# All matrix products of a three-layer network as whole float32 matmuls, with weights packed tile by tile

## The chip, the cores and the metric

The kernel runs on one core of a Trainium2 chip. The metric is the device time of one execution in microseconds (us). Before the change it is 1247.71 us, the median of 3 runs (1245.24 to 1251.49).

## The reference, cut to what matters

All data is float32: 256 tokens of width 1024, batch 1. There are seven sublayers; numbered by `s` in the kernel they are 0 to 6:

```
s=0 mixer_ab:  proj = h @ w_in_ab  (1024 x 2072); sparse + window attention, sink attention; y = o @ w_out
s=1, 3 ffn:    y = (silu(h @ w_gate) * (h @ w_up)) @ w_down          (1024 x 2816 twice, 2816 x 1024)
s=2 mixer_cd:  proj = h @ w_in_cd  (1024 x 2304); block attention, stick-breaking attention; y = o @ w_out
s=4, 6 ffn:    the same with other weights, residual factor 0.5
s=5 mixer_s5:  proj = h @ w_in_2   (1024 x 2048); gated convolution and a state space with a gate; y = o @ w_out_2
around each:   h = rms_norm(x) * (1 + scale) + shift;   x = x + gate * (norm of) y
               scale, shift, gate = c @ mod_w + mod_b    (21 vectors of 1024, each from a 1024 x 1024 matrix)
```

The products accumulate over a depth of 1024 (8 tiles of 128), in the last product of a feed-forward part over 2816 (22 tiles).

## The kernel before, in words

The activations `h` stay in SBUF, feature-major: 8 tiles of 128 features by 256 tokens. All weights are streamed once from HBM. SyncE issues nearly all loads on one queue, in order; a load waits there until its buffer is free. TensorE's instructions stand in the program's written order. The other engines' order is found by the framework's planner.

**Three passes.** Most products are made from parts. `split` (L170) takes a raw weight tile of 128x1024 and makes a high part `whi` on ScalarE (L184, type fp32r) and the rest, `wlo`, on VectorE (L185). `evac` (L110) does the same with the activations, as `hhi` and `hlo`. Then `mm3` (L100 to L108) adds three matmuls of fp32r operands: high by high, high by low, low by high. One call of `mm3` with low parts is thus three matmul instructions, of 128 stationary columns and 256 moving ones in the projections (`proj_a`, L225). `out_step` (L439) does the same with 512 moving columns in the feed-forward parts' last product (L449 to L451), and `tok_half` (L470) with token-major products (L480, L483).

**Whole products already there.** Where there are no low parts the operands are plain float32 and one matmul call is made: the attention mixers' output projections (L447, operands `raw` and `o`: 2 mixers x 8 depth tiles x 2 halves of the rows x 2 halves of the columns = 64 calls of 512 columns), the convolution's 12 column tiles in `mixer_s5` (L104, `h` and `raw`: 12 x 8 = 96 calls of 256 columns), the gate of the state space (L1529: 16 calls of 256 columns), its first inputs (L1360: 64 calls of 128 columns).

**Calls in three passes.** With 256 columns: the feed-forward parts' projections, 4 parts x 20 column tiles x 2 matrices x 8 = 1280, the projections of `mixer_ab` and `mixer_cd`, 13 column tiles x 8 = 104 each, together 1488; and the token-major first columns of the feed-forward parts, 4 x 2 halves x 2 matrices x 8 = 128. With 512 columns: 4 parts x 22 x 2 x 2 = 352 in the last products, 16 in `mixer_cd`, 16 in `mixer_s5`.

**Modulations.** `mod` (L285) accumulates `c @ mod_w` on VectorE, row tile by row tile (L252, tile `macc`), as background work that `plan` and `pay` (L138 to L152) spread over the feed-forward parts. `mod_part` (L261) splits the sum, and `mod_end` (L270) sums it over partitions with two matmuls of 512 columns (L276, L277); 19 vectors in two halves make 38.

**Buffers.** 4 raw weight buffers of 8 KB a partition, 4 of 4 KB for the modulations (`mraw`), 4 each of 4 KB for `whi` and `wlo`. Weights are loaded by columns, in runs of 512 to 2048 bytes, or by rows, in runs of 2048 or 4096. `chain` (L214) prepares one item (load and split) ahead of the item that runs.

**Boundaries.** At the end of a feed-forward part (`out_halves`, L516) the last four depth tiles run for the first half of the tokens, then for the second; under the second, the first half's norm is made and transposed (L365). `split_ahead` (L499) splits the next part's first weights.

Of the kernel before, what the change touches and what calls it, by code (L numbers as in the profile page):

```python
# [61 lines left out]

class Net:
    def __init__(self, ctx, tc, I, out, dbg=None):
        self.ctx, self.tc, self.nc, self.I, self.out, self.dbg = ctx, tc, tc.nc, I, out, dbg or {}
        self.bgq, self.late, self.wait = [], [], 0
        self.anchor = None
        self.nacc = 0
        self.nextra = 0
# [30 lines left out]
    def mm3(self, out, lh, ll, rh, rl, first, last):  # L100
        """float32 product: in three passes over parts, or, without low parts, as it is"""
        mm = self.nc.tensor.matmul
        if ll is None:
            mm(out, lh, rh, start=first, stop=last)  # L104
            return
        mm(out, lh, rh, start=first, stop=False)  # L106
        mm(out, lh, rl, start=False, stop=False)  # L107
        mm(out, ll, rh, start=False, stop=last)  # L108

    def evac(self, hi, lo, ps, scale=None):  # L110
        nc = self.nc
        if lo is None:
            nc.scalar.activation(hi, ps, AF.Copy, scale=1.0 if scale is None else scale)  # L113
        else:
# [23 lines left out]
    def plan(self, slots):  # L138
        """the waiting work, by its time, over steps of the given slack"""
# [26 lines left out]
    # ---------------------------------------------------------------- weights  # L166
    def raw(self):
        return self.wp.tile([128, 2048], F32, tag="raw", name="raw", bufs=4)

    def split(self, src, shape, pool=None):  # L170
        n = 1
        for s in shape:
            n *= s
        p, bufs = (self.wp, 4) if pool is None else (pool, self.nextra)
        hi = p.tile([128, 1024], F32R, tag="whi", name="whi", bufs=bufs)
        lo = p.tile([128, 1024], F32R, tag="wlo", name="wlo", bufs=bufs)

        def view(t):
            v = t[:, :n]
            if len(shape) == 2:  # L180
                return v.rearrange("p (a b) -> p a b", a=shape[0])
            return v.rearrange("p (a b c) -> p a b c", a=shape[0], b=shape[1])
        hv, lv = view(hi), view(lo)
        self.nc.scalar.activation(hv, src, AF.Copy)  # L184
        self.nc.vector.tensor_tensor(lv, src, hv.bitcast(F32), ALU.subtract)  # L185
        if len(shape) == 3:
            hv = hi[:, :n].rearrange("p (a b) -> p a b", a=shape[0])
            lv = lo[:, :n].rearrange("p (a b) -> p a b", a=shape[0])
        return hv, lv

    def load_cols(self, w, cols):
        """[1024, n] columns (a list of (start, stop)) -> raw [128, 8, total]"""
        tot = sum(b - a for a, b in cols)
        r = self.raw()
        v = r[:, :8 * tot].rearrange("p (k n) -> p k n", k=8)
        o = 0
        for a, b in cols:
            self.nc.sync.dma_start(out=v[:, :, o:o + b - a],
                                   in_=w[:, a:b].rearrange("(k p) n -> p k n", p=128))
            o += b - a  # L200
        return v

    def load_rows(self, w, r0, c0, c1):
        """rows r0 .. r0 + 511 of some columns -> raw [128, 4, n]"""
        r = self.raw()[:, :4 * (c1 - c0)].rearrange("p (k n) -> p k n", k=4)
        self.nc.sync.dma_start(out=r, in_=w[r0:r0 + 512, c0:c1].rearrange("(k p) n -> p k n", p=128))
        return r

    def weights(self, src, shape, xl, pool=None):
        """the weights as a product with x takes them: in parts if x is in parts"""  # L210
        return (src, None) if xl is None else self.split(src, shape, pool)
# [22 lines left out]
    def mod_start(self, w, b, c, grain):  # L234
        """b + c @ w, as partial sums over 128 partitions"""
# [7 lines left out]
        nc.sync.dma_start(out=acc[0:1, :], in_=b)  # L243
        wv = w.rearrange("(p k) n -> p k n", p=128)

        def piece(i):
            def run():
                for kk in range(grain * i, grain * i + grain):
                    r = self.wp.tile([128, D], F32, tag="mraw", name="mraw", bufs=4)
                    nc.sync.dma_start(out=r, in_=wv[:, kk, :])  # L250
                    with self.behind(kk == 0):
                        nc.vector.scalar_tensor_tensor(acc, r, c[:, kk:kk + 1], acc, ALU.mult, ALU.add)  # L252
            return run
        return acc, [piece(i) for i in range(8 // grain)]

    def behind(self, on):
        """behind the last part's norm on the vector engine"""
# [3 lines left out]
    def mod_part(self, acc, b):  # L261
        nc = self.nc
        sl = slice(512 * b, 512 * b + 512)
        hi = self.mp.tile([128, 512], F32R, tag="mhi", name="mhi", bufs=1)
        lo = self.mp.tile([128, 512], F32R, tag="mlo", name="mlo", bufs=1)
        nc.scalar.activation(hi, acc[:, sl], AF.Copy)
        nc.vector.tensor_tensor(lo, acc[:, sl], hi.bitcast(F32), ALU.subtract)  # L267
        return hi, lo

    def mod_end(self, b, part, kind, arg, dst):  # L270
        """sum over partitions, for all partitions: dst [128, 1024]"""
        nc = self.nc
        hi, lo = part
        sl = slice(512 * b, 512 * b + 512)
# [10 lines left out]
    def mod(self, key, w, b, c, kind, arg, row=None, grain=2):  # L285
        """queue the work on one modulation vector; the result is self.m[key]"""
        box = {}

        def start():
            box["acc"], box["pieces"] = self.mod_start(w, b, c, grain)  # L290
# [7 lines left out]
        def end(b):  # L298
            if b > 0:
                if b == 1:  # L300
                    box["dst"] = (self.mp.tile([128, D], F32, tag="mod", name="mod", bufs=3) if row is None
                                  else box["acc"])
                self.mod_end(b - 1, box["part"], kind, box["arg"], box["dst"])
                if row is None:
                    self.m[key] = box["dst"]
                elif b == 2:
                    self.nc.sync.dma_start(out=row, in_=box["acc"][0:1, :])
            if b < 2:
                box["part"] = self.mod_part(box["acc"], b)
        n = 8 // grain  # L310
        items = [start] + [lambda i=i: box["pieces"][i]() for i in range(1, n)] + [lambda b=b: end(b) for b in range(3)]
        lag, after = LAGS.get(self.s, (LAG, LAG))

        def part():
            self.tick(True)
            end(0)

        def last():
            end(1)
            self.late.append([after, lambda: end(2)])  # L320
        return [(1.25 * grain, f) for f in items[:n]] + [(0.7, part)] + ([(lag, None)] if lag else []) + [(1.4, last)]
# [1494 lines left out]
```

## Time and profile before

| what | value |
|---|---|
| median of 3 runs | 1247.71 us |
| span of the profiled execution (first to last instruction; the page gives no other time of it) | 1248.2 us |
| TensorE matmul busy | 1177.6 us, 94% |
| TensorE weight load busy | 1019.2 us, 82% |
| VectorE, ScalarE, GpSimd busy | 919.5, 611.5, 136.9 us |
| moved by DMA | 304.38 MB, mean 244 GB/s |
| `split`: `whi` on ScalarE, `wlo` on VectorE, 308 times each | 318.4 us, 368.6 us |

A matmul's record lasts longer than the distance to the next one's start, since matmuls overlap in the array: what a product costs in a stream is read from starts, not from durations.

### The profile page before, as it was taken

How to read it: one execution, taken by the hardware profiler on the slowest of the kernel's cores; microseconds unless marked ns; L12 is line 12 of the kernel's file. 1: busy time of each engine (PE TensorE's matmuls, PEld its weight loads, DVE VectorE, ACT ScalarE, POOL GpSimd, SP SyncE). 2: the span in 40 equal slices, each digit the busy share in tenths (PEclk: the TensorE clock that was granted, in tenths of full speed). 3: DMA queues.
4: the chain of work that ended last, by engine and by line, in shares of the span. 5: the costliest groups of instructions: out<-in, count | busy, mean ns of one | idle time of the engine just before them, and what ended most of it. 6: DMA issues, size and time to landing. Idle time of an engine off the chain costs nothing.

```text
span 1248.2 us, 19610 instructions
## 1 busy us (share of the span) xinstructions
PE 1177.6 (94%) x7475; PEld 1019.2 (82%) x7475; DVE 919.5 (74%) x1378; ACT 611.5 (49%) x1110; POOL 136.9 (11%) x182
## 2 busy tenths in 40 slices
PE   6897999999999969899999989999999979999997
PEld 2795658999887955699998789998888747999986
DVE  6786839877758677796985699789559978755545
ACT  2364635445444645454454546776642423544433
POOL 2000000000001003100100010000007951000000
PEclk9997999999999989999999999999999989999999
DMA  9999498968965979798887479789665465755540
GB/s 341 309 277 274 121 283 277 355 211 298 349 227 154 271 242 232 247 342 296 295 314 264 161 242 353 244 314 364 230 201 152 154 211 168 227 165 183 203 169 34
DMA packets 203629, 304.38 MB, mean 244 GB/s; under 512 B 18423, under 2 KB 153331, under 8 KB 203534
## 3 DMA queue, kind: packets, MB, share of 16 engines
q1 hardware_dynamic: 203534, 303.12, 74.7%
q8 instruction: 59, 0.97, 0.3%
q14 instruction: 36, 0.29, 0.1%
HBM read 295.97 MB, written 7.11 MB: 243 GB/s over the span
## 4 chain that ended last, share of the span: by engine, by line
PE 35%; issue 17%; DVE 6%; POOL 3%; ACT 2%; DMA 1%; POOLq 0%; SPq 0%; DVEq 0%; ACTq 0%
PE ps L108 6%; PE ps L106 6%; PE ps L107 6%; PE y L451 3%; PE y L449 3%; PE y L450 3%; PE y L447 2%; PE tok L480 1%; PE ps L1360 1%; DVE st L1412 1%; DVE wlo L185 1%; PE glu L1529 1%; POOL xt L1404 1%; DVE ue L1080 1%; PE ps L365 1%
## 5 line engine op out<-in xcount | busy, mean ns | idle before, releaser
L184 ACT ACTIVATE whi<-raw 128x1024 fp32r<-128x1024 f32 (+2 forms) x308 | 318.4, 1042 | 398.5 <-PE ps L107 158.2
L185 DVE TENSOR_TENSOR wlo<-raw,whi 128x1024 fp32r<-128x1024 f32 (+2 forms) x308 | 368.6, 1204 | 179.1 <-ACT whi L184 178.4
L106 PE MATMUL ps<-hhi,whi 128*128 128x256 f32 x1488 | 424.7, 285 | 1.5 <-DVE st L611 1.5
L108 PE MATMUL ps<-hhi,wlo 128*128 128x256 f32 x1488 | 422.3, 284 | 4.0 <-DVE wlo L185 4.0
L107 PE MATMUL ps<-hlo,whi 128*128 128x256 f32 x1488 | 421.9, 284 | 0.0
L108 PEld LDWEIGHTS ps<-hhi,wlo 128*128 128x128 f32 x1488 | 286.3, 192 | 5.1 <-DVE wlo L185 5.1
L106 PEld LDWEIGHTS ps<-hhi,whi 128*128 128x128 f32 x1488 | 286.3, 192 | 4.2 <-DVE st L611 1.7
L107 PEld LDWEIGHTS ps<-hlo,whi 128*128 128x128 f32 x1488 | 286.4, 192 | 1.4 <-DVE wlo L185 0.5
L252 DVE SCALAR_TENSOR_TENSOR macc<-mraw,c,macc 128x1024 f32<-128x1024 f32 x152 | 194.4, 1280 | 19.4 <-DMA mraw<-in_mod_w_dram 8.5
L449 PE MATMUL y<-whi,gh 128*128 128x512 f32 x352 | 139.7, 397 | 0.0
L450 PE MATMUL y<-wlo,gh 128*128 128x512 f32 x352 | 138.9, 395 | 0.0
L451 PE MATMUL y<-whi,gl 128*128 128x512 f32 x352 | 138.9, 395 | 0.0
L242 POOL MEMSET macc<- 128x1024 f32 x19 | 18.3, 962 | 557.6 <-DVE mlo L267 540.7
L451 PEld LDWEIGHTS y<-whi,gl 128*128 128x128 f32 x352 | 66.1, 188 | 15.8
L450 PEld LDWEIGHTS y<-wlo,gh 128*128 128x128 f32 x352 | 66.2, 188 | 15.4
L449 PEld LDWEIGHTS y<-whi,gh 128*128 128x128 f32 x352 | 66.1, 188 | 15.2
L447 PE MATMUL y<-raw,o 128*128 128x512 f32 x128 | 57.4, 596 | 0.7 <-ACT o L113 0.7
L332 POOL TENSOR_SCALAR ms<-ss 128x1 f32<-128x1 f32 x24 | 11.6, 482 | 372.8 <-ACT junk L342 368.9
L555 DVE TENSOR_TENSOR g<-sg,ps 128x256 f32<-128x256 f32 x80 | 33.3, 416 | 23.0 <-PE ps L108 22.5
L447 PEld LDWEIGHTS y<-raw,o 128*128 128x128 f32 x128 | 23.4, 190 | 27.3 <-issue 25.6
L104 PE MATMUL ps<-h,raw 128*128 128x256 f32 x192 | 43.7, 382 | 1.8 <-DVE cvt L1490 1.8
L618 ACT ACTIVATE p<-p,st 128x128 f32<-128x128 f32 (+1 forms) x64 | 28.4, 444 | 30.3 <-DVE st L611 24.6
(335 smaller groups left out, 1505.5 us busy)
## 6 DMA issues: line engine op xcount, KB each, us to landing
raw<-in_ffn_w_in_dram SPq DMA_DIRECT2D x44, 1024.0 KB
mraw<-in_mod_w_dram SPq DMA_DIRECT2D x80, 512.0 KB
mraw<-in_w_mod_dram SPq DMA_DIRECT2D x72, 512.0 KB
raw<-in_ffn_w_out_dram SPq DMA_DIRECT2D x22, 1024.0 KB
raw<-in_ffn_w_gate_dram SPq DMA_DIRECT2D x22, 1024.0 KB
raw<-in_ffn_w_up_dram SPq DMA_DIRECT2D x22, 1024.0 KB
raw<-in_ffn_w_down_dram SPq DMA_DIRECT2D x22, 1024.0 KB
raw<-in_w_out_ab_dram SPq DMA_DIRECT2D x16, 512.0 KB
```

What stands on the lines that cost most here:

```text
L104: mm(out, lh, rh, start=first, stop=last)
L106: mm(out, lh, rh, start=first, stop=False)
L107: mm(out, lh, rl, start=False, stop=False)
L108: mm(out, ll, rh, start=False, stop=last)
L184: self.nc.scalar.activation(hv, src, AF.Copy)
L185: self.nc.vector.tensor_tensor(lv, src, hv.bitcast(F32), ALU.subtract)
L252: nc.vector.scalar_tensor_tensor(acc, r, c[:, kk:kk + 1], acc, ALU.mult, ALU.add)
L447: mm(ys[h][b], xh[:, k, c], wh[:, 0, sl], start=first, stop=last)
L449: mm(ys[h][b], xh[:, k, c], wh[:, 0, sl], start=first, stop=False)
L450: mm(ys[h][b], xh[:, k, c], wl[:, 0, sl], start=False, stop=False)
L451: mm(ys[h][b], xl[:, k, c], wh[:, 0, sl], start=False, stop=last)
L555: nc.vector.tensor_tensor(g, sg, pu, ALU.mult)
```

## The change

Every product becomes one matmul call with plain float32 operands. `mm3`, `split`, `mod_part` and `split_ahead` go, with the high and low parts of weights, activations and modulation sums. The host packs the weights into tiles in which each partition's data is contiguous (up to 8192 bytes) and `load` fetches one tile with one DMA. All weights, the modulations' among them (two row tiles in one buffer), share one ring of 10 buffers of 8 KB (`RING`). A buffer is now free again when the matmuls (for modulations: VectorE) have read it, not when it has been split. At a feed-forward part's end six depth tiles in place of four (`PAIRS` = 3) run half of the rows after half.

```diff
+RING, PAIRS = 10, 3
-EXTRA = {1: 2}
-    def mm3(self, out, lh, ll, rh, rl, first, last):
-        mm(out, lh, rh, start=first, stop=False)
-        mm(out, lh, rl, start=False, stop=False)
-        mm(out, ll, rh, start=False, stop=last)
-    def evac(self, hi, lo, ps, scale=None):
-            nc.scalar.activation(hi, ps, AF.Copy)
-            return nc.vector.tensor_tensor(lo, ps, hi.bitcast(F32), ALU.subtract).ins
+    def evac(self, out, ps, scale=1.0):
+        self.nc.scalar.activation(out, ps, AF.Copy, scale=scale)
     def raw(self):
-        return self.wp.tile([128, 2048], F32, tag="raw", name="raw", bufs=4)
-    def split(self, src, shape, pool=None):
-        self.nc.scalar.activation(hv, src, AF.Copy)
-        self.nc.vector.tensor_tensor(lv, src, hv.bitcast(F32), ALU.subtract)
+        return self.wp.tile([128, 2048], F32, tag="raw", name="raw", bufs=RING)
+    def load(self, src):
+        n = src.shape[1:]
+        r = self.raw()[:, :math.prod(n)]
...
+        self.nc.sync.dma_start(out=v, in_=src)
         return v
-    def proj_a(self, w, xh, xl):
+    def proj_a(self, w, x):
         ps = self.bank([256])
         for k in range(8):
-            self.mm3(ps, w[0][:, k, :], None if xl is None else w[1][:, k, :], xh[:, k, :],
-                     None if xl is None else xl[:, k, :], k == 0, k == 7)
+            self.nc.tensor.matmul(ps, w[:, k], x[:, k, :], start=k == 0, stop=k == 7)
         return ps
 @@ mod_start
-                    r = self.wp.tile([128, D], F32, tag="mraw", name="mraw", bufs=4)
-                    nc.sync.dma_start(out=r, in_=wv[:, kk, :])
+                    if kk % 2 == 0:
+                        box["r"] = self.load(self.I["mod"][i - 2, kk // 2])
 @@ mod_end
-        nc.tensor.matmul(ps, self.ones_r, hi, start=True, stop=False)
-        nc.tensor.matmul(ps, self.ones_r, lo, start=False, stop=True)
+        nc.tensor.matmul(ps, self.ones, acc[:, sl], start=True, stop=True)
 @@ out_step
-                mm(ys[h][b], xh[:, k, c], wh[:, 0, sl], start=first, stop=False)
-                mm(ys[h][b], xh[:, k, c], wl[:, 0, sl], start=False, stop=False)
-                mm(ys[h][b], xl[:, k, c], wh[:, 0, sl], start=False, stop=last)
+                self.nc.tensor.matmul(ys[h][b], x[:, k, c], w[:, 512 * b:512 * b + 512], start=first, stop=last)
 @@ out_halves
-        joint = nk // 2 - 2
+        joint = nk // 2 - PAIRS
 @@ ffn
-                    g = gated(pg, pu)
-                    nc.scalar.activation(gh[:, f, :], g, AF.Copy)
-                    nc.vector.tensor_tensor(gl[:, f, :], g, gh[:, f, :].bitcast(F32), ALU.subtract)
+                    gated(pg, pu, gh[:, f, :])
 @@ mixer_s5, bmm
-                        self.mm3(ps[n][:, x, :], bh[rows, 4 * x + j], bl[rows, 4 * x + j], uh[rows, j], ul[rows, j], True, True)
+                        nc.tensor.matmul(ps[n][:, x, :], bm[rows, x, j], u[rows, j], start=True, stop=True)
```

## Rows read from the trace of the kernel before

**Rows 1.** The page's parts 1 and 2: TensorE's busy time, granted clock by slice.
```profile
PE 1177.6 (94%) x7475; PEld 1019.2 (82%) x7475; DVE 919.5 (74%) x1378; ACT 611.5 (49%) x1110; POOL 136.9 (11%) x182
...
PEclk9997999999999989999999999999999989999999
```

**Rows 2.** Windows, one for each of s = 0 to 6: busy us (count), clock, DMA.
```profile
0.00:187.00 187.00, 162.74 (x790) 112.80 (x790) 124.33 (x323) 86.88 (x230) 12.24 (x24) 0.94 0.92 267
187.00:388.00 201.00, 196.84 (x1357) 182.83 (x1356) 154.78 (x179) 98.25 (x145) 7.59 (x12) 0.99 0.80 273
388.00:513.00 125.00, 113.21 (x648) 85.88 (x648) 89.86 (x136) 64.56 (x146) 15.16 (x23) 0.96 0.87 245
513.00:719.00 206.00, 200.29 (x1379) 185.17 (x1378) 160.66 (x238) 102.34 (x158) 14.28 (x15) 0.99 0.79 272
719.00:919.00 200.00, 195.75 (x1356) 181.13 (x1355) 167.06 (x213) 126.07 (x206) 7.82 (x10) 1.00 0.82 282
919.00:1048.00 129.00, 117.12 (x616) 92.80 (x616) 104.30 (x153) 45.27 (x102) 77.03 (x92) 0.97 0.53 175
1048.00:1249.00 201.00, 191.69 (x1339) 178.64 (x1337) 118.48 (x142) 88.09 (x127) 2.75 (x6) 0.99 0.50 168
```

**Rows 3.** Waits of the splitting engine: who for whom, us, times, longest.
```profile
ACT whi L184 <- PE ps L107: 158.2, 114, 2.0
ACT whi L184 <- PE y L451: 107.7, 67, 4.6
```

**Rows 4.** Matmul groups by line and shape: count | busy us, mean ns | idle before.
```profile
L106 PE MATMUL ps<-hhi,whi 128*128 128x256 f32 x1488 | 424.7, 285 | 1.5 <-DVE st L611 1.5
...
L449 PE MATMUL y<-whi,gh 128*128 128x512 f32 x352 | 139.7, 397 | 0.0
...
L447 PE MATMUL y<-raw,o 128*128 128x512 f32 x128 | 57.4, 596 | 0.7 <-ACT o L113 0.7
L104 PE MATMUL ps<-h,raw 128*128 128x256 f32 x192 | 43.7, 382 | 1.8 <-DVE cvt L1490 1.8
...
L276 PE MATMUL ps<-mhi,ones_r 128*128 128x512 f32 x38 | 18.0, 473 | 7.9 <-ACT mhi L266 7.9
```

**Rows 5.** Timeline of matmuls near 300 us (start us, us): one product to the next.
```profile
299.76 0.28 PE L106 MATMUL ps<-hhi,whi 128*128 128x256 f32 x1
...
300.12 0.28 PE L106 MATMUL ps<-hhi,whi 128*128 128x256 f32 x1
```

**Rows 6.** Timeline of matmuls near 880 us: one product of 512 columns to the next.
```profile
879.86 0.39 PE L449 MATMUL y<-whi,gh 128*128 128x512 f32 x1
...
880.56 0.40 PE L449 MATMUL y<-whi,gh 128*128 128x512 f32 x1
```

**Rows 7.** The chain that ended last, 496 to 520 us: start us, us, what.
```profile
497.31 0.23 PE ps L276
497.54 0.23 PE ps L277
...
499.50 10.30 PE y L447 x24
```

**Rows 8.** The same chain, 1010 to 1030 us.
```profile
1022.43 3.47 PE glu L1529 x16
```

**Rows 9.** Weight loads by line and shape: count | busy us, mean ns | idle before.
```profile
L106 PEld LDWEIGHTS ps<-hhi,whi 128*128 128x128 f32 x1488 | 286.3, 192 | 4.2 <-DVE st L611 1.7 <-issue 1.4 <-ACT whi L184 0.2
...
L104 PEld LDWEIGHTS ps<-h,raw 128*128 128x128 f32 x192 | 36.0, 190 | 7.3 <-DVE cvt L1490 2.0
```

**Rows 10.** Waits of TensorE alone: us, times, longest.
```profile
PE ps L365 <- DVE ht L357: 10.8, 8, 3.5
PE ps L276 <- ACT mhi L266: 7.9, 1, 7.9
...
PE ps L1003 <- DVE zr L1001: 5.6, 1, 5.6
PE ps L108 <- DVE wlo L185: 4.0, 5, 1.7
```

More of the change, by code (lines that the diff above doesn't have):

```diff
@@ L167, in raw @@
     def raw(self):
-        return self.wp.tile([128, 2048], F32, tag="raw", name="raw", bufs=4)
-    def split(self, src, shape, pool=None):
[L171 to L183, printed above, removed]
-        self.nc.scalar.activation(hv, src, AF.Copy)
-        self.nc.vector.tensor_tensor(lv, src, hv.bitcast(F32), ALU.subtract)
[L186 to L200, printed above, removed]
-        return v
[L203 to L211, printed above, removed]
+        return self.wp.tile([128, 2048], F32, tag="raw", name="raw", bufs=RING)
+    def load(self, src):
+        n = src.shape[1:]
+        r = self.raw()[:, :math.prod(n)]
+        if len(n) == 1:
+            v = r
+        elif len(n) == 2:
+            v = r.rearrange("p (a b) -> p a b", a=n[0])
+        else:
+            v = r.rearrange("p (a b c) -> p a b c", a=n[0], b=n[1])
+        self.nc.sync.dma_start(out=v, in_=src)
+        return v
     @staticmethod
@@ L298, in end, with last @@
         def end(b):
[L299 to L309, printed above, removed]
+            if b == 0:
+                box["dst"] = (self.mp.tile([128, D], F32, tag="mod", name="mod", bufs=3) if row is None
+                              else box["acc"])
+            self.mod_end(b, box["acc"], kind, box["arg"], box["dst"])
+            if row is None:
+                self.m[key] = box["dst"]
+            elif b == 1:
+                self.nc.sync.dma_start(out=row, in_=box["acc"][0:1, :])
         n = 8 // grain
-        items = [start] + [lambda i=i: box["pieces"][i]() for i in range(1, n)] + [lambda b=b: end(b) for b in range(3)]
+        items = [start] + [lambda i=i: box["pieces"][i]() for i in range(1, n)]
         lag, after = LAGS.get(self.s, (LAG, LAG))
-        def part():
-            self.tick(True)
+        def last():
             end(0)
[L318 to L321, printed above, removed]
+            self.late.append([after, lambda: end(1)])
+        return ([(1.25 * grain, f) for f in items] + [(0.1, lambda: self.tick(True))] +
+                ([(lag, None)] if lag else []) + [(1.4, last)])
     def rstd(self, ss, extra=None):
@@ L436, in after, with out_step @@
             nc.sync.dma_start(out=self.out[0, 128 * h:128 * h + 128, sl], in_=t)
-    def out_step(self, ys, halves, w, k, xh, xl, first, last, bs=(0, 1)):
-        mm = self.nc.tensor.matmul
+    def out_step(self, ys, halves, w, k, x, first, last, bs=(0, 1)):
         for h in halves:
@@ L443, in out_step, with out_items @@
             for b in bs:
-                sl = slice(512 * b, 512 * b + 512)
-                wh, wl = w
-                if xl is None:
-                    mm(ys[h][b], xh[:, k, c], wh[:, 0, sl], start=first, stop=last)
-                    continue
-                mm(ys[h][b], xh[:, k, c], wh[:, 0, sl], start=first, stop=False)
-                mm(ys[h][b], xh[:, k, c], wl[:, 0, sl], start=False, stop=False)
-                mm(ys[h][b], xl[:, k, c], wh[:, 0, sl], start=False, stop=last)
-    def out_items(self, ys, halves, loads, ks, nk, xh, xl, keep=None, pool=None):
+                self.nc.tensor.matmul(ys[h][b], x[:, k, c], w[:, 512 * b:512 * b + 512], start=first, stop=last)
+    def out_items(self, ys, halves, w, ks, nk, x, keep=None):
         def prepare(i):
-            r = self.raw().rearrange("p (k n) -> p k n", k=2)
-            loads(i, r)
-            return [self.weights(r[:, k:k + 1, :], [1, 1024], xl, pool if 2 * i + k >= nk - self.nextra else None) for k in range(2)]
+            r = self.load(w[i])
+            return [r[:, k] for k in range(2)]
         def run(i, ws):
@@ L478, in tok_half, with ahead @@
             for k in range(8):
-                for x in range(2):
-                    mm(p, xh[:, k, c], w[k // n][x][:, k % n, :], start=k == 0 and x == 0, stop=False)
-        for p, w in zip(ps, ws):
-            for k in range(8):
-                mm(p, xl[:, k, c], w[k // n][0][:, k % n, :], start=False, stop=k == 7)
+                self.nc.tensor.matmul(p, x[:, k, c], w[k // n][:, k % n, :], start=k == 0, stop=k == 7)
         return ps
-    def ahead(self, n=2):
+    def ahead(self):
@@ L488, in ahead @@
         s, I = self.s + 1, self.I
         if s == 5:
-            us = [self.load_cols(I["w_in_2"][0], [(1536 + 256 * i, 1792 + 256 * i)]) for i in range(2)]
-            self.first = lambda: us
+            us = [self.load(I["s5_u"][i]) for i in range(2)]
         elif s == 2:
-            rs = [self.load_rows(I["w_in_cd"][0], 512 * i, 1792, 2304) for i in range(2)]
-            self.split_ahead([(r[:, 2 * i:2 * i + 2, :], [2, 512]) for r in rs for i in range(2)], n)
+            us = [self.load(I["cd_vd"][i]) for i in range(2)]
@@ L495, in ahead @@
         elif s < 7:
-            rs = [self.load_cols(w, [(0, 256)]) for w in self.ffn_weights(s)[:2]]
-            self.split_ahead([(r[:, 4 * i:4 * i + 4, :], [4, 256]) for r in rs for i in range(2)], n)
-    def split_ahead(self, parts, n):
-        ws = [self.split(*a) for a in parts[:n]]
-        def more(m=3):
-            with self.tc.issue_after(self.anchor):
-                ws.extend(self.split(*a) for a in parts[n:m])
-        self.more = more
-        self.first = lambda: ws + [self.split(*a) for a in parts[len(ws):]]
@@ L508, in ffn_weights @@
-    def ffn_weights(self, s):
-        I = self.I
-        if s < 4:
-            w = I["ffn_w_in"][s // 2]
-            return w[:, :DFF], w[:, DFF:], I["ffn_w_out"][s // 2]
-        n = "ffn1" if s == 4 else "ffn2"
-        return I[n + "_w_gate_2"][0], I[n + "_w_up_2"][0], I[n + "_w_down_2"][0]
-    def out_halves(self, loads, nk, xh, xl, s):
+            us = [self.load(w[0]) for w in self.ffn_weights(s)[:2]]
+        else:
+            us = None
+        self.first = lambda: us
+    def ffn_weights(self, s):
+        n = (1, 3, 4, 6).index(s)
+        return [self.I[f"ffn_{x}{n}"] for x in "gud"]
@@ L556, in gated @@
                 return g
[L558 to L559 removed]
+            ws = [[w] for w in self.first()]
+            g0 = gated(*self.tok_half(0, ws, hh))
             self.second()
[L561 removed]
+            g1 = gated(*self.tok_half(1, ws, hh))
             def turned(h, g):
@@ L750, in run, with a_items, tok_items @@
             for k in range(4):
-                self.mm3(ps[t], ws[0][:, k, :], ws[1][:, k, :], hh[:, 4 * i + k, :], hl[:, 4 * i + k, :],
-                         i == 0 and k == 0, i == 1 and k == 3)
+                self.nc.tensor.matmul(ps[t], raw[i][:, k, t], hh[:, 4 * i + k, :], start=i == 0 and k == 0, stop=i == 1 and k == 3)
             return ps[t]
-        return prepare, run
-    def a_items(self, w, cols, hh, hl, put):
+        return run
+    def a_items(self, w, hh, put):
         box = {}
+        each = w.shape[2]
         def prepare(n):
-            if n % 2 == 0:
-                box["v"] = self.load_cols(w, [(a, a + 128) for a in cols[n:n + 2]])
-            return self.weights(box["v"][:, :, 128 * (n % 2):128 * (n % 2) + 128], [8, 128], hl)
+            if n % each == 0:
+                box["v"] = self.load(w[n // each])
+            return box["v"][:, n % each]
         def run(n, ws):
-            put(n, self.proj_a(ws, hh, hl))
+            put(n, self.proj_a(ws, hh))
             self.bg()
-        return [(lambda n=n: prepare(n), lambda ws, n=n: run(n, ws)) for n in range(len(cols))]
-    def tok_items(self, w, cols, hh, hl, v, extra=None):
-        n = sum(b - a for a, b in cols)
-        nk = 4
+        return [(lambda n=n: prepare(n), lambda ws, n=n: run(n, ws)) for n in range(each * w.shape[0])]
+    def tok_items(self, w, hh, v, extra=None):
+        n, nk = w.shape[3], w.shape[2]
         nk2 = min(nk, 1024 // n)
@@ L778, in prepare @@
             if k0 % nk == 0:
-                r = self.raw()[:, :nk * n].rearrange("p (k n) -> p k n", k=nk)
-                box["r"] = r
-                o = 0
-                for a, b in cols:
-                    self.nc.sync.dma_start(out=r[:, :, o:o + b - a],
-                                           in_=w[128 * k0:128 * (k0 + nk), a:b].rearrange("(k p) n -> p k n", p=128))
-                    o += b - a
+                box["r"] = self.load(w[k0 // nk])
             k1 = k0 % nk
-            return self.split(box["r"][:, k1:k1 + nk2, :], [nk2, n])
+            return box["r"][:, k1:k1 + nk2, :]
         def run(k0, ws):
-            wh, wl = ws
-            mm = self.nc.tensor.matmul
             if k0 == 0:
@@ L850, in gates @@
                 nc.vector.reciprocal(gt, gt)
-            tok = self.tok_items(w, [(896, 1024), (1152, 1304), (1944, 2072)], hh, hl, v, gates)
-            prepare, run = self.early
-            first = [(lambda t=t: prepare(1, t), lambda ws, t=t: self.evac(qb[:, t, :], None, run(1, t, ws), 0.125))
-                     for t in range(4)]
-            first += self.a_items(w, [1816], hh, hl, lambda n, ps: self.evac(kb, None, ps))
+            tok = self.tok_items(I["ab_v"], hh, v, gates)
+            first = [(lambda: None, lambda ws, t=t: self.evac(qb[:, t, :], self.early(1, t), 0.125)) for t in range(4)]
+            first += self.a_items(I["ab_kb"], hh, lambda n, ps: self.evac(kb, ps))
             later, self.bgq = self.bgq, []
@@ L913, in mixer_ab @@
             self.pipeline(units, fill, bg=(6, 12))
-            self.finish(0, ya, self.out_items(yb, (1,), loads, range(4), 8, o8, None), yb)
+            self.finish(0, ya, self.out_items(yb, (1,), loads, range(4), 8, o8), yb)
     def finish(self, s, ya, items, yb):
@@ L1434, in ymm @@
                 for x in range(2):
-                    self.mm3(yps[j], zs[:, i4, x], None, xt[:, x], None, i4 == 0 and x == 0, i4 == 3 and x == 1)
+                    nc.tensor.matmul(yps[j], zs[:, i4, x], xt[:, x], start=i4 == 0 and x == 0, stop=i4 == 3 and x == 1)
                 if i4 == 3:
@@ L1513, in end @@
                     into_x(h, ys[h], cst["r"])
-                return self.chain(self.out_items(ys, (h,), loads(0), range(2), 4, ch, None)) + [end]
+                return self.chain(self.out_items(ys, (h,), I["s5_out"], range(2), 4, ch)) + [end]
             gl = {}
             def glu_load():
-                gl["w"] = []
-                for i in range(2):
-                    t = self.wp.tile([128, D], F32, tag="mraw", name="gluw", bufs=4).rearrange("p (k n) -> p k n", k=2)
-                    nc.sync.dma_start(out=t, in_=I["glu_w_2"][0, 256 * i:256 * i + 256, :].rearrange("(k p) n -> p k n", p=128))
-                    gl["w"] += [t[:, 0], t[:, 1]]
+                w = self.load(I["s5_glu"][0])
+                gl["w"] = [w[:, k] for k in range(4)]
             def glu(k):
@@ L1550, in mixer_s5 @@
             glu(3)
-            sh = [ap.tile([128, 4, 256], F32R, name="sh" + x, **k) for x, k in (("h", {"tag": "zs"}), ("l", {}))]
+            sh = ap.tile([128, 4, 256], F32, name="sh", tag="zs")
             for f in range(4):
@@ L1560, in mixer_s5 @@
             ys, kept = {}, []
-            for f in self.chain(self.out_items(ys, (0,), loads(512), range(2), 4, *sh, kept)):
+            for f in self.chain(self.out_items(ys, (0,), I["s5_out"][2:4], range(2), 4, sh, kept)):
                 f()
@@ L1669, in start @@
             self.bias_rows(*bias)
-            self.early = prepare, run = self.q_halves(I["w_in_ab"][0], 1304, hh, hl)
-            early = {}
-            with self.tc.issue_after(self.anchor):
-                early = {t: prepare(0, t) for t in range(4)}
+            run = self.early = self.q_halves(I["ab_qb"], hh)
             load(1, 0, 0)
             load(1, 0, 1)
-            run(0, 0, early[0])
-            run(0, 1, early[1])
+            run(0, 0)
+            run(0, 1)
             scaled(1, tb)
@@ L1749, in run @@
                     self.bgq += extra[k]()
-            hh, hl = self.h
+            hh = self.h
             if s == 0:
-                self.dump("h0", hh.bitcast(F32))
+                self.dump("h0", hh)
             if s == 0:
-                self.mixer_ab(hh, hl)
+                self.mixer_ab(hh)
             elif s == 2:
-                self.mixer_cd(hh, hl)
+                self.mixer_cd(hh)
             elif s == 5:
-                self.mixer_s5(hh, hl)
+                self.mixer_s5(hh)
                 stack.close()
```

329 lines of the change are left out of this document (137 added, 192 removed).

## The prediction

> **What bounds the kernel now.** I read the page's busy times first. TensorE's matmuls are busy for 94% of the span and no other engine for more than 74% [rows 1]: 1248.2 - 1177.6 leaves 70.6 us in which TensorE does nothing, and that is all that a change elsewhere could take away. Then the windows by part: in the four feed-forward parts (201, 206, 200 and 201 us, 808 of the 1248) TensorE is busy for 95 to 98% at a clock of 0.99 or 1.00, while VectorE has 33 to 83 us to spare in each and DMA is at half to 0.82 of its time; in the three mixers (187, 125, 129 us) TensorE still has 87 to 91% [rows 2]. Then who waits for whom. The step that the change removes, the split, is not late: ScalarE, which makes the high part, waits 158.2 us for the third matmul of the projections and 107.7 us for that of the last products, that is for a split buffer to come free [rows 3]. In the other direction TensorE waits 4.0 us in all for a low part in the projections [rows 10]. So TensorE's own stream sets the pace, and the question is what one product costs on it.
>
> **What a product costs, in three passes and whole.** Busy time misleads here, since records overlap; I count starts.
> - Three passes, 256 columns: from one product's first matmul to the next one's, 300.12 - 299.76 = 0.36 us [rows 5]; three records.
> - Three passes, 512 columns: 880.56 - 879.86 = 0.70 us [rows 6].
> - Whole, 512 columns: 24 records in 10.30 us, 0.429 us each [rows 7].
> - Whole, 256 columns: 16 records in 3.47 us, 0.217 us each [rows 8].
>
> A whole product's record is thus nearly twice as long as a pass of a split one (0.217 against 0.12). What decides is how many records it has. The code calls L447 with `raw` and `o` 64 times and the trace has 128 records; it calls L104 with `h` and `raw` 96 times and the trace has 192 [rows 4]. For the split products the counts agree: 1488 calls, 1488 records of L106; 352 and 352 of L449 [rows 4]. So one whole float32 matmul call goes to the array as two matmuls, each of them at half the speed of an fp32r pass. It costs 2 x 0.217 = 0.434 us for 256 columns, where three passes cost 0.36, and 2 x 0.429 = 0.858 us for 512, where three passes cost 0.70. The change makes the bounding engine's work longer by about a fifth.
>
> **The sum, part by part.**
> - 256 columns: 1488 products in L106 to L108 and 128 token-major ones, 1616 x (0.434 - 0.36) = 119.6 us more.
> - 512 columns: 352 + 16 + 16 = 384 products x (0.858 - 0.70) = 60.7 us more.
> - Modulation sums: 38 [rows 4], today two matmuls of 0.23 us each [rows 7], then 0.858 us: 38 x 0.40 = 15.1 us more.
> - The token-major products of 408 and 128 columns and the state space's products from 32 rows: no row gives these whole. By width the first get longer by some 2 us, the second shorter by some 2; I take 0, bounds -3 and +4.
>
> That is 195 us more on TensorE. Against it stands what can be gained:
> - The split, the parts of the activations and of the modulation sums leave VectorE and ScalarE. In the feed-forward parts this is worth nothing by itself, since those engines wait for TensorE. Of TensorE's idle time the 4.0 us for low parts go. The 5.6 us for L1003, queued on VectorE behind splits, should mostly go. The 10.8 us for the normed halves (L365) shrink: at a feed-forward part's end six depth tiles instead of four now lie under the first half's norm, 12 x 0.858 = 10.3 us in place of 8 x 0.70 = 5.6. The 7.9 us for a modulation sum (L276) may stay: the split goes, but the matmul then waits directly for VectorE's last accumulation, and all of TensorE's queue stands behind it. I take 28 us of the 70.6 as gone; bounds 4 and 58, the latter if nothing is left but the first load and the last norm, some 13 us together.
> - The granted clock: 1 minus the clock, times the length, summed over the seven windows, is 26 us [rows 2]. It is low where TensorE pauses, in the mixers. A stream that pauses less gets some of it back: I take 13, bounds 0 and 26 (partly the same time as the idle above).
> - The packed loads. DMA moves 267 to 282 GB/s in the first five parts, at 0.79 to 0.92 of its time [rows 2], and these parts get longer, so demand per microsecond falls. Better runs can only shorten waits that are in the 70.6 us. I take nothing extra.
> - A new wait: a raw buffer is now held until its matmuls have run, and modulations share the ring, so a load that waits for its buffer holds all loads behind it on SyncE. In a feed-forward part a pair of column tiles is 2 MB and lasts 32 x 0.434 = 13.9 us on TensorE, 151 GB/s; the modulations come on top, which makes the 273 GB/s of s = 1 some 273 x 201 / 242 = 227. Ten buffers hold five such pairs, about 70 us of work less what modulations hold. I take 0; bounds 0 and 40 us (a fifth of one feed-forward part's weights landing late, in each of the four parts).
>
> 1248 + 195 - 28 - 13 = 1402 us. The profiled span and the median of the runs differ by 0.5 us, so I forecast the same for the median: 1402.
>
> One rule of the Trainium skill speaks for a still longer stream. TensorE's weight loads have mean records of 192 ns for an fp32r stationary and 190 for a float32 one [rows 9], and both lie under the matmuls of the streams counted above. The Trainium skill ("TensorE: Matmul & The Clock Gate", section "Weight-path perf modes — Fast Weight Load (FWL) and DoubleRow") says that the fast weight load is not used for FP32 weights, which would make the split's loads the cheaper ones. The trace doesn't agree: 192 against 190 ns. It also gives, under "LDWEIGHTS (loading the stationary operand)", columns / 1.2 ns, by which an estimate is 107 ns for 128 columns; if that were exposed before each of the 2 x 2038 records, 435 us more would follow.
>
> **Rivals.**
> 1. *Waits eat more.* The shared ring runs dry, or TensorE waits for modulation sums in the mixers. For it: the wait of 7.9 us exists today [rows 10], and modulations are accumulated on VectorE in turn with the softmax. Against it: VectorE loses its largest job and the ring is deeper. Time: no gain at all (1443) and up to 40 us more, 1443 to 1483. Chance 0.09.
> 2. *Idle goes almost wholly.* 58 us of idle and the clock's 26 us less an overlap: 1248 + 195 - 75 = 1368 or a little below. For it: VectorE and ScalarE get so much free time that the softmax and scan chains of the mixers run ahead. Against it: those chains are steps in a row and stay as they are. Chance 0.06 for less than 1365.
> 3. *The other side: a packed whole product needs one record.* The mechanism is that the second record is not the product's own, or not needed when the tile is contiguous; its place is every stream of products; it decides as soon as a product of 256 columns costs under 0.36 us. At one record: 1616 x (0.217 - 0.36) + 384 x (0.429 - 0.70) = -335 us, 913 on TensorE, where DMA would then bound: the windows' lengths times their rates are 304 MB, at the 282 GB/s of s = 4 1079 us [rows 2]. Against it: 128 records for 64 calls and 192 for 96 [rows 4], the latter with weights in a raw tile as they would come now. Chance 0.03.
> 4. *Weight loads show.* If the 190 ns of a load [rows 9] stood beside each record, 2 x 2038 x 0.19 = 774 us more, about 2180. Against it: 24 records of L447 at 0.429 us with loads between them [rows 7]. Chance 0.01.
>
> **How the numbers follow.** The forecast has 0.81. Its own range is 1365 to 1443: at the low end 58 us of idle gone and the clock's share, at the high end nothing gained. Case 1 overlaps above, so the range given is 1362 to 1450, with cases 2, 3, 4 and most of 1 outside. About 0.5% is what a measurement of this kernel can tell from no change (6 us). Faster by more than that needs case 3: 0.03. Within it: 0.01, if gains that I don't see meet the 195 us. Slower: 0.96.
>
> **What would show it.** Matmul records of proj_a's line: 2 x 1488 + 192, starts 0.216 apart; the last products' starts 0.43 apart. Feed-forward windows of 238 to 246 us, with TensorE at 97% or more. `mixer_ab` with the start 185 to 195 us, `mixer_cd` 125 to 135, `mixer_s5` 118 to 128. VectorE busy below 551 us (919.5 less the split's 368.6), no `wlo`. TensorE's waits for L365 at half of today's. The prediction is wrong if starts in the new stream are closer than 0.18 us (case 3), if TensorE's idle time is above 75 us (case 1), or if a feed-forward part is under 230 us.

## The result and the profile after

The changed kernel takes 1410.27 us, the median of 4 runs (1408.95 to 1411.0), against 1248.01 us of the kernel before, now the median of 4 runs; the ratio is 1.1295, 95% interval 1.1272 to 1.1318. The forecast was 1402 us, within 1362 to 1450. The profiled execution has a span of 1407.8 us.

The page's busy times and granted clock, as [rows 1] had them:

```profile
PE 1356.9 (96%) x5411; PEld 968.5 (69%) x5411; DVE 505.6 (36%) x910; ACT 264.1 (19%) x679; POOL 132.2 (9%) x182
...
PEclk9898999999999999999999999999999999999999
```

VectorE lost 414 us of work and ScalarE 347, and the profiled execution is 160 us longer (1407.8 against 1248.2): TensorE has 179 us more. The windows by part, with the columns of [rows 2]:

```profile
0.00:202.00 202.00, 171.23 (x669) 109.23 (x670) 97.68 (x287) 66.43 (x201) 12.19 (x24) 0.93 0.76 269
202.00:439.00 237.00, 236.75 (x917) 172.24 (x916) 65.25 (x77) 19.65 (x49) 7.57 (x12) 1.00 0.59 219
439.00:567.00 128.00, 124.00 (x514) 83.79 (x514) 63.78 (x108) 46.21 (x125) 16.13 (x23) 0.97 0.74 264
567.00:808.00 241.00, 239.43 (x935) 173.77 (x934) 73.99 (x138) 24.46 (x60) 14.13 (x15) 1.00 0.61 222
808.00:1045.00 237.00, 236.75 (x918) 172.21 (x917) 82.31 (x114) 54.16 (x114) 6.55 (x10) 1.00 0.64 237
1045.00:1169.00 124.00, 118.11 (x571) 88.63 (x570) 89.51 (x137) 34.78 (x88) 73.08 (x92) 1.00 0.55 191
1169.00:1408.00 239.00, 230.62 (x896) 168.67 (x894) 33.11 (x51) 18.43 (x43) 2.59 (x6) 0.99 0.38 128
```

The feed-forward parts go from 201, 206, 200 and 201 us to 237, 241, 237 and 239: 146 of the 160 us, with TensorE busy for all but 0.2 to 8.4 us of each. `mixer_ab` with the start takes 15 us more, `mixer_cd` 3 more, `mixer_s5` 5 less. The matmul groups that answer to [rows 4] (L236 is `proj_a`, L430 `out_step`):

```profile
L236 PE MATMUL ps<-h,raw 128*128 128x256 f32 x3104 | 677.6, 379 | 1.5 <-DVE cvt L1365 1.5
L430 PE MATMUL y<-raw,gh 128*128 128x512 f32 x704 | 306.4, 592 | 0.0
...
L272 PE MATMUL ps<-macc,ones 128*128 128x512 f32 x76 | 40.4, 613 | 3.5 <-issue 3.5
```

Every count is doubled: 704 records for 352 calls, 76 for 38, and 3104 for 1552 calls of `proj_a` (1456 that were split, since 32 early query products have a line of their own, and the convolution's 96). Two stretches of the timeline of TensorE give the pace, to set beside [rows 5, 6]:

```profile
299.65 2.32 PE L236 MATMUL ps<-h,raw 128*128 128x256 f32 x10
...
424.65 2.74 PE L430 MATMUL y<-raw,gh 128*128 128x512 f32 x6
```

Ten records in 2.32 us less the last one's own 0.379 are (2.32 - 0.379) / 9 = 0.216 us from start to start, 0.431 per product. Six in 2.74 are (2.74 - 0.592) / 5 = 0.430, 0.859 per product. Last, TensorE's waits, as in [rows 10]:

```profile
PE ps L1555 <- DMA pe<-in_nsa_cmp_pe_dram: 8.9, 1, 8.9
PE ps L938 <- DVE pc L931: 8.7, 1, 8.7
...
PE ps L354 <- DVE ht L346: 1.5, 1, 1.5
```

The wait for the normed halves fell from 10.8 to 1.5 us, and those for the split are gone. Two are long now: 8.7 us for the compressed probabilities (L938), which is new, and 8.9 us for a load of 8 KB, the position embeddings `pe`. The first product on `pe` (L1697 in the kernel before) waited there too, but less, and the trace puts that wait down to a load beside it:

```profile
PE ps L1697 <- DMA mraw<-in_mod_w_dram: 2.8, 1, 2.8
```

### The profile page after: what moved, and what is told of

Read it like the earlier page. It is cut to its first block, busy times and chain, and to the rows that moved or that the text cites. A ratio compares the mean times of both kernels' runs of the same rounds, so it can differ in the third digit from the quotient of the medians.

```text
span 1407.8 us, 14024 instructions
## 1 busy us (share of the span) xinstructions
PE 1356.9 (96%) x5411; PEld 968.5 (69%) x5411; DVE 505.6 (36%) x910; ACT 264.1 (19%) x679; POOL 132.2 (9%) x182
## 4 chain that ended last, share of the span: by engine, by line
PE 44%; issue 18%; DVE 3%; POOL 3%; ACT 1%; DMA 0%; POOLq 0%; SPq 0%; DVEq 0%; ACTq 0%
PE ps L236 23%; PE y L430 13%; PE tok L455 2%; PE ps L272 1%; POOL xt L1284 1%; DVE st L1292 1%; PE ps L1247 1%; POOL xt L1285 0%; PE glu L1395 0%; DVE ue L971 0%; DMA ct<-cmat 0%; POOL xs L1305 0%; PE ps L354 0%; DVE q L1283 0%; PE ps L545 0%
## 5 line engine op out<-in xcount | busy, mean ns | idle before, releaser
L236 PE MATMUL ps<-h,raw 128*128 128x256 f32 x3104 | 677.6, 379 | 1.5 <-DVE cvt L1365 1.5
L236 PEld LDWEIGHTS ps<-h,raw 128*128 128x128 f32 x3104 | 588.0, 190 | 88.9 <-issue 7.5
L430 PE MATMUL y<-raw,gh 128*128 128x512 f32 x704 | 306.4, 592 | 0.0
L430 PEld LDWEIGHTS y<-raw,gh 128*128 128x128 f32 x704 | 133.1, 190 | 163.6 <-issue 163.4
L258 DVE SCALAR_TENSOR_TENSOR macc<-raw,c,macc 128x1024 f32<-128x1024 f32 x152 | 195.0, 1283 | 84.4 <-DMA raw<-in_mod_dram 57.8
L507 DVE TENSOR_TENSOR gh<-sg,ps 128x256 f32<-128x256 f32 x80 | 33.6, 420 | 357.4 <-PE ps L236 357.4
L506 ACT ACTIVATE sg<-ps 128x256 f32<-128x256 f32 x80 | 30.5, 381 | 432.3 <-PE ps L236 424.4
L455 PE MATMUL tok<-raw,h 128*128 128x256 f32 (+1 forms) x288 | 71.1, 404 | 1.2 <-ACT h L153 1.1
L455 PEld LDWEIGHTS tok<-raw,h 128*128 128x128 f32 x288 | 54.3, 190 | 17.7 <-issue 9.1
L430 PE MATMUL y<-raw,o 128*128 128x512 f32 x128 | 57.4, 596 | 0.4 <-ACT o L153 0.4
L272 PE MATMUL ps<-macc,ones 128*128 128x512 f32 x76 | 40.4, 613 | 3.5 <-issue 3.5
L430 PEld LDWEIGHTS y<-raw,o 128*128 128x128 f32 x128 | 23.4, 190 | 28.2 <-issue 26.5
```

Of the source, the lines that this page charges most:

```text
L236: self.nc.tensor.matmul(ps, w[:, k], x[:, k, :], start=k == 0, stop=k == 7)
L258: nc.vector.scalar_tensor_tensor(acc, box["r"][:, kk % 2], c[:, kk:kk + 1], acc, ALU.mult, ALU.add)
L272: nc.tensor.matmul(ps, self.ones, acc[:, sl], start=True, stop=True)
L430: self.nc.tensor.matmul(ys[h][b], x[:, k, c], w[:, 512 * b:512 * b + 512], start=first, stop=last)
L455: self.nc.tensor.matmul(p, x[:, k, c], w[k // n][:, k % n, :], start=k == 0, stop=k == 7)
L506: nc.scalar.activation(sg, pg, AF.Silu)
```

## The experiments

**The two halves of the change, one by one.** The theory: TensorE pays for whole products, and everything else is small. The rival: the packed loads, the ring and their order on the queue cost the time. The first kernel is the one before with packed weights:

```diff
-                rg = self.load_cols(wg, [(256 * c, 256 * c + 256)])
-                ru = self.load_cols(wu, [(256 * c, 256 * c + 256)])
+                rg, ru = self.load(wg[c]), self.load(wu[c])
...
-            r = self.raw().rearrange("p (k n) -> p k n", k=2)
-            loads(i, r)
+            r = self.load(loads[i])
```

> The kernel before with one part of the change alone: the weights of the projections and output products packed by the host and fetched tile by tile; the three passes, the split, the buffers and the modulations' loads are as before. Theory (TensorE pays for whole products, the packing is nearly free): 1235 to 1250 us, three-pass products still 0.36 and 0.70 us apart, any gain only from TensorE's waits for loads at the start, some 12 us in all. Rival (the packed loads and their order on the queue cost the time): above 1300 us.

Measured: 1226.14 us, ratio 0.9839 (0.9804 to 0.9873). The rival is out, and so is the size in my expectation: packing is a gain of 20 us. Its windows for s = 0, 1 and 2:

```profile
0.00:175.00 175.00, 157.47 (x789) 110.67 (x790) 124.94 (x324) 88.16 (x231) 12.22 (x24) 0.96 0.83 286
175.00:374.00 199.00, 195.97 (x1360) 182.04 (x1359) 154.44 (x178) 97.34 (x145) 7.78 (x14) 1.00 0.75 276
374.00:491.00 117.00, 111.45 (x648) 84.20 (x647) 90.86 (x137) 66.80 (x150) 14.94 (x22) 1.00 0.77 266
```

Against [rows 2] `mixer_ab` loses 12 us and `mixer_cd` 8; the feed-forward part only 2. In the two mixers many weights came in runs of 512 bytes: DMA then moved 267 GB/s at 0.92 of its time in s = 0, now 286 at 0.83. TensorE's waits show where the gain lands. The 5.6 us of L1003 in `mixer_ab` are gone, and the 7.9 us for a modulation sum in `mixer_cd` [rows 10] are 1.6 (line 314 of this kernel). By the order of the rows both stand at the end of a chain that begins with a late load: before L1003, VectorE had waited 8.7 us for the tile `T` (now 0.8), and before the modulation sum 7.4 us for a bias row of 4 KB. The wait for `T`, VectorE's longest from 80 to 113 us of the kernel before:

```profile
DVE tcb L1016 <- DMA T<-rd: 8.7, 1, 8.7
```

The second kernel is the one before with whole products and its old loads. It has 8 raw buffers in place of 4, the modulation sums stay in two passes, and of the weights only the queries' tiles come packed:

```diff
     def split(self, src, shape, pool=None):
-        self.nc.scalar.activation(hv, src, AF.Copy)
-        self.nc.vector.tensor_tensor(lv, src, hv.bitcast(F32), ALU.subtract)
+        return src, None
     def raw(self):
-        return self.wp.tile([128, 2048], F32, tag="raw", name="raw", bufs=4)
+        return self.wp.tile([128, 2048], F32, tag="raw", name="raw", bufs=8)
```

> [...] Theory: as the changed kernel less the 38 modulation sums (15 us) and less the 9 us wait that the changed kernel has at 53 us: 1380 to 1400 us, two records of 0.216 and 0.429 us per product. Rival (packing and ring cost the time): below 1300 us.

Measured: 1411.94 us, ratio 1.1334 (1.1298 to 1.137): whole products, without packing and ring, are enough for a loss of the same size. The time is 12 us above my upper end. I took the wait for `pe` to belong to the ring of the changed kernel; it is here too, with 8 raw buffers, as TensorE's longest wait. I also gave the old loads no cost: s = 0 takes 212 us here, 10 more than in the changed kernel.

```profile
PE ps L1671 <- DMA pe<-in_nsa_cmp_pe_dram: 10.8, 1, 10.8
```

**TensorE's stream as the pace of the kernel before.** The kernel before without the second and third pass:

```diff
-        mm(out, lh, rh, start=first, stop=False)
-        mm(out, lh, rl, start=False, stop=False)
-        mm(out, ll, rh, start=False, stop=last)
+        mm(out, lh, rh, start=first, stop=last)
```

> The kernel before, leaving out the second and third pass of all split products (so its outputs lack those terms); the split itself, with high and low parts, is still made. Theory (TensorE's stream sets the pace, the split is hidden): 1616 x 0.24 + 384 x 0.47 = 568 us leave TensorE; then VectorE (919 us busy before) and DMA bound it: 960 to 1080 us. Rival (the split on ScalarE and VectorE paces the feed-forward parts): 1200 us or more, with TensorE waiting for low and high parts.

Measured: 1065.47 us in two runs, ratio 0.8552 (0.8514 to 0.859): the split, made in full, did not hold the kernel at 1248. What bounds next is the split or the loads, which this run does not tell apart. The waits of this kernel (all engines, longest totals) show TensorE waiting for high parts, as it did not before, and ScalarE waiting for raw weights to make them from. A window from 200 to 700 us shows VectorE busy for 91% of it and DMA at 0.96:

```profile
PE ps L106 <- ACT whi L182: 77.2, 46, 5.4
ACT whi L182 <- DMA raw<-in_ffn_w_in_dram: 60.0, 28, 10.0
```

```profile
200.00:700.00 500.00, 350.62 (x1784) 288.18 (x1784) 455.30 (x618) 293.53 (x502) 41.95 (x51) 0.81 0.96 318
```

**One term by itself.** The changed kernel (with PAIRS = 2 and 6 buffers, to make room) with the feed-forward parts' last products alone back in three passes:

```diff
-                self.nc.tensor.matmul(ys[h][b], x[:, k, c], w[:, 512 * b:512 * b + 512], start=first, stop=last)
+                    mm(ys[h][b], x[0][:, k, c], w[0][:, sl], start=first, stop=False)
+                    mm(ys[h][b], x[0][:, k, c], w[1][:, sl], start=False, stop=False)
+                    mm(ys[h][b], x[1][:, k, c], w[0][:, sl], start=False, stop=last)
```

> The changed kernel with a ring of 6 and PAIRS = 2 (1396.8 us), and one class of products back in three passes: the feed-forward parts' last ones, 352 of 512 columns, with weights and activations split on ScalarE and VectorE. Theory (each whole product of 512 columns costs 0.858 us and three passes 0.70, and the split hides): 352 x 0.158 = 55.6 us less, 1337 to 1346 us. Rival (the split's two steps stand before the products, as there is little run-ahead): 1360 us or more, TensorE waiting for low parts.

Measured: 1342.38 us, ratio 1.0769 (1.0745 to 1.0792), 54.4 us below the same kernel with whole products (1396.83): 0.155 us for each of 352 products, where the starts gave 0.158. The split of weights and activations added nothing that shows: among TensorE's waits is none for a high or a low part, and the three passes are there once for each of the 352 products.

```profile
L440 PE MATMUL y<-whi,gh 128*128 128x512 f32 x352 | 146.3, 416 | 0.0
```

**The new wait.** The changed kernel once more, as the measure of the runs beside it:

> The changed kernel once more, as the measure for the three runs beside it: 1405 to 1414 us.

It took 1409.81 us. Then the small load moved to the first constants:

```diff
+            self.pe = cp.tile([32, 64], F32, name="pe")
+            nc.sync.dma_start(out=self.pe, in_=I["nsa_cmp_pe"][0])
...
-        pe = ap.tile([32, 64], F32, name="pe")
-        nc.sync.dma_start(out=pe, in_=I["nsa_cmp_pe"][0])
+        pe = self.pe
```

> The changed kernel with one small load moved: the 8 KB of position embeddings are fetched among the first constants, not after the weights that the ring of ten already has in flight. Theory (the wait of 9 us at 53 us is this load's place behind some 6 MB on the DMA queue): that wait gone, 1398 to 1404 us, a ratio of 0.993 to 0.996 to the changed kernel. Rival (TensorE would wait there for something else anyway, the products behind it need weights that land no earlier): within 2 us of it.

Measured: 1403.56 us, ratio to the kernel before 1.1249 (1.1223 to 1.1275): 6.3 us less, as expected, with runs from 1400.06 to 1407.71. The next two change one constant each.

```diff
-RING, PAIRS = 10, 3
+RING, PAIRS = 10, 2
```

> The changed kernel with PAIRS = 2: four depth tiles instead of six run half of the rows after half at a feed-forward part's end. Theory (the cover of 10.3 us under the norm took most of TensorE's waits for L365): cover 6.9 us, still above the 5.6 of before; 0 to 2 us more at each of three boundaries, 1408 to 1416 us. Rival (the cover is worth nothing): within 1 us of the changed kernel, waits for the normed half no longer.

Measured: 1409.74 us, no difference from 1409.81. The time lies in both ranges; TensorE's waits for the normed half, 2.0 us in place of 1.5, speak for the rival.

```diff
-RING, PAIRS = 10, 2
+RING, PAIRS = 6, 2
```

> As the run with PAIRS = 2, and a ring of 6 buffers in place of 10. Theory (the ring is deeper than TensorE needs, and depth only makes small loads wait at the start): the same within 5 us, the wait at 53 us shorter. Rival (the ring runs dry): 20 to 40 us more, TensorE waiting for raw tiles in the feed-forward parts.

Measured: 1396.83 us, ratio 1.1192 (1.1168 to 1.1217), 13 us less than with ten buffers. I had expected the same time within 5 us: a ring of ten is not only more than needed, it costs. SyncE's queue shows how. The changed kernel (start us, us; each row is one or more issues):

```profile
28.86 1.60 SPq L217 DMA_DIRECT2D raw<-in_ab_v_dram  x2
30.51 0.43 SPq L217 DMA_DIRECT2D raw<-in_ab_cmp_dram  x1
...
33.97 2.87 SPq L217 DMA_DIRECT2D raw<-in_mod_dram  x2
37.79 0.33 SPq L217 DMA_DIRECT2D raw<-in_ab_qa_dram  x1
39.82 0.68 SPq L730 DMA_DIRECT2D rd<-ma  x1
41.84 0.33 SPq L217 DMA_DIRECT2D raw<-in_mod_dram  x1
44.38 0.33 SPq L752 DMA_DIRECT2D sink<-in_swa_sinks_dram  x1
44.76 2.67 SPq L1553 DMA_DIRECT2D pe<-in_nsa_cmp_pe_dram  x1
```

The same with 6 buffers:

```profile
29.83 0.33 SPq L217 DMA_DIRECT2D raw<-in_ab_v_dram  x1
...
32.39 0.69 SPq L730 DMA_DIRECT2D rd<-ma  x1
33.66 0.34 SPq L217 DMA_DIRECT2D raw<-in_ab_cmp_dram  x1
40.58 0.33 SPq L752 DMA_DIRECT2D sink<-in_swa_sinks_dram  x1
40.96 4.58 SPq L1553 DMA_DIRECT2D pe<-in_nsa_cmp_pe_dram  x1
```

With ten buffers three modulation tiles and a query tile, 4 MB that TensorE does not need yet, are issued ahead of `pe`, and its product starts at 62.8 us; with six they come behind it and the product starts at 52.5 without a wait. No row gives the landing of `pe` itself; that it stood behind the 4 MB is read from the order of issues and from the two runs in which the wait is gone. Both edits together:

> The changed kernel with a ring of 6, PAIRS = 2, and the small load moved to the start as well. Theory (both edits take away the same wait, that of the small load behind what the ring has in flight): no more than 2 us below the ring of 6 alone, 1394 to 1398 us. Rival (they are two waits): 1386 to 1391 us.

Measured: 1398.32 us, ratio 1.1212 (1.1189 to 1.1235), the same as the ring of 6 alone: with six buffers, moving `pe` gains nothing more. Yet one edit is not worth the other. The ring of 6 alone (1396.83) is 6.7 us below the moved load in a ring of ten (1403.56), so it takes away something besides this wait. The two profiled executions differ by 3.4 us, and what it is was not separated.

**The version that beats both.** Packed loads with three passes are already faster than both kernels. With the small load moved as well:

> The three-pass kernel with packed loads (1226 us, ratio 0.984), and the small load of position embeddings moved among the first constants. Theory (that load's place on the queue costs TensorE 3.9 us there): 1220 to 1224 us. Rival (the wait moves to the weights behind it): 1225 to 1227 us.

Measured: 1225.22 us, ratio 0.9822 (0.9802 to 0.9843), not to be told from 1226.14: the rival. The wait of 3.9 us is gone from the trace, one of 2.0 us stands behind it at the next product, and what is left of the gain is within the scatter of the runs.

## Why the prediction was right, point by point

- *TensorE's stream sets the pace; the split hides.* Shown from both sides: taking passes away with the split kept gave 0.8552, and bringing the split back for one class of products cost nothing that shows and gained 54.4 us. One reading was off and changes nothing: L107 is the second of the three matmuls, the last that reads `whi`, not the third.
- *A whole product is two records at half the speed of an fp32r pass.* Shown: counts 704 for 352 and 76 for 38, starts 0.216 and 0.430 us apart. The terms: 256 columns 1616 x (0.431 - 0.36) = 115 us (forecast 119.6, from the 0.217 for a record in the row of the chain); 512 columns 60.7 forecast, and 0.155 in place of 0.158 for each in the run that isolates 352 of them; modulation sums 76 x 0.43 - 38 x 0.46 = 15.2 (15.1).
- *Idle time.* I took 28 us of the 70.6 as gone; 1407.8 - 1356.9 = 50.9 are left, so 20 went. L365's wait shrank more than I thought (10.8 to 1.5). My reason, the third pair of depth tiles, doesn't hold: with two pairs it is 2.0. What remains as a cause is that each product under the norm lasts longer and VectorE is free for it; that was not separated. The 5.6 us of L1003 went too, but my reason, splits queued ahead on VectorE, was wrong: VectorE had waited for the tile `T`, and packed loads take this wait away with every split in place. Two waits in `mixer_ab` took their place: 6.1 us more for `pe`, and 8.7 us for the compressed probabilities (L938), where VectorE has four modulation accumulations of 1.28 us between the short steps of the softmax from 132.8 to 140.7 us. In the kernel before none stands between the same steps (125.1 to 129.5 us). The run with whole products and old loads has no such wait, so whole products alone don't make it. That the planner's new order put the accumulations there was not tried by a run.
- *The granted clock.* (1 - 0.98) x 1248 = 25 us before, (1 - 0.987) x 1408 = 18 after: 7 us back, where I took 13. In s = 0 it even fell, from 0.94 to 0.93, in the part with the new waits.
- *The new wait on the queue.* I took 0, bounds 0 and 40. TensorE waits 8.9 us, 6.1 more than before. Moving the load gave 6.3 us, the ring of 6 gave 13. The pause costs more than itself: from 62.7 to 76.8 us the granted clock is 0.85, and the 32 records of L711 take 12.6 us, in the ring of 6 without the pause 11.2 at a clock of 1.00. The place is not the one I named, feed-forward parts whose ring runs dry (TensorE idles for 0.2 us in two of them), but the start. And the cause is the reverse: not a load that waits for its buffer, but many buffers free, so that loads are issued early and stand ahead of a small one.
- *The packed loads.* I took nothing, on the ground that they can only shorten waits that are in the 70.6 us. That is the step that failed most. Alone they give 20 us, in the mixers. In the profiled execution of that run TensorE's idle time is 55.1 us, 15 less, but its busy time fell by 9 as well (1177.6 to 1168.8, the granted clock 0.980 to 0.989), and those 9 did not lie in the 70.6. Of the idle time that I put down to the missing split, part is thus the packing's. In the changed kernel the ring of ten costs 13 us against one of six.
- *Rivals.* Waits that eat more: there, but 6 to 13 us at the start and 8.7 for L938, and they did not use up what was gained. One record per product: out by the counts. Weight loads showing: out by the starts. Of the windows forecast, `mixer_ab` missed (202 for 185 to 195), two feed-forward parts lie 1 us below their range, and in the last one TensorE is busy for 96.5%, not 97.

The signed sum: 115 + 61 + 15 of stream, less 20 of idle and 7 of clock, is 164 us; the spans differ by 159.6. I took the stream 4 us too long and the gains 14 us too high, which makes 1412 of the forecast's 1402; no row gives the place of the 4 us by which that is above the span. That the total came so near is partly luck. I left out a gain, the packing, and two losses in `mixer_ab`, the waits for `pe` and of L938, and they have opposite signs.

The Trainium skill ("FP8 and Floating Point Precision", section "TensorE Precision Notes") says that true FP32 takes four passes through the array. The trace agrees in the time, about: a whole product takes 0.431 us for 256 columns and 0.859 for 512, which is 3.6 and 3.7 times the 0.12 and 0.233 of an fp32r pass of the kernel before. It shows two records, not four; that each holds two of the passes is not shown.

## What to carry to other kernels

Where TensorE is the bound, price a change of operand type by starts and by records per call, not by mean durations or by the number of calls in the code: one whole float32 call in place of three fp32r calls looked like a saving and cost 20 to 23% on the products counted here (0.431 for 0.36 us, 0.859 for 0.70). Work that leaves idle engines is worth nothing until it is what others wait for. And a deeper prefetch ring is not always better: here, with ten buffers in place of six, big loads that nobody needed yet stood in front of a small one that the next product needed.

## What the hardware showed that I had not expected

- Packing changed how the same data came: DMA packets under 2 KB fell from 153331 to 21731, all packets from 203629 to 76251, at 304 MB both times. In s = 0 DMA moved 267 GB/s at 0.92 of its time before, packed 286 at 0.83, the same data in 12 us less. The run lengths and the number of loads changed together, and no run separates the two.
- In the run with one pass, TensorE was busy for 70% of 200 to 700 us, with pauses between, and its mean granted clock was 0.81 there, between the levels of 1.2 and 2.4 GHz, where the kernel before has 0.99 to 1.00 in its feed-forward parts. Part of the remaining passes thus ran at the lower level. Behind a pause of 4.97 us, 8 records take 2.08 us at a granted clock of 0.50; after one of 0.27 us, 24 take 3.12 at 1.00:

```profile
522.12 2.08 PE L106 MATMUL ps<-hhi,whi 128*128 128x256 f32 x8 [4.97 <-ACT whi L182]
214.72 3.12 PE L106 MATMUL ps<-hhi,whi 128*128 128x256 f32 x24 [0.27 <-ACT whi L182]
```
